# Attention scores in two stacked 128-row passes and four 32-row products per pair of q tiles

## The chip, the core and the metric

The kernel runs on one core of a Trainium2 chip. The metric is the time of one execution on the device in microseconds (us), the median of several runs. The engines are named as in the profile: PE multiplies matrices (PEld is its load of the stationary operand), DVE and ACT work on vectors, POOL does slower vector work, SP issues DMAs. They run side by side, each through its own queue in order, and wait for each other at semaphores.

## What is computed

A two-layer encoder of 1024 tokens and width 1024. Each layer has a mixer (latent attention of 8 heads beside a gated convolution module) and a gated feed-forward part with a short convolution. The change touches the attention:

```python
def block(args):
    qn, qr = args
    sc = (jnp.einsum("bqhd,bkhd->bhqk", qn, k_nope)
          + jnp.einsum("bqhr,bkr->bhqk", qr, k_rope))
    p = jax.nn.softmax(sc.astype(jnp.float32) * scale, axis=-1).astype(v.dtype)
    return jnp.einsum("bhqk,bkhd->bqhd", p, v)
```

`q_nope` and `k_nope` have 64 values a head, the rotary parts `q_rope` and `k_rope` 32, and `k_rope` is shared by the heads; values have 64.

## The kernel before

**Halves.** A 32-bit operand goes to PE as two 16-bit halves, a high one and the rest ("hi", "lo"), and a product is the sum of three: hi·hi, hi·lo, lo·hi. A query or key tile of a head is `(128, 2, 1024)`: 96 of its 128 partitions are used (64 nope, 32 rope), axis 1 is the half, and the last axis are the tokens.

**A q tile.** The attention of a layer (`attention`, L1781) takes the 8 heads × 8 blocks of 128 queries as 64 steps. For a step:

- `scores` (L1818): six products of 96 rows and 512 columns fill a score tile `s` of two PSUM banks (1024 keys); then DVE takes the negated maximum `mx` of each row (L1820).
- `expo` (L1828): ACT writes `p`, the exponential, and its row sum. In the profile it is an ACTIVATE and an ACTIVATION_READ_ACCUMULATOR.
- `turn` (L1858): PE transposes blocks of 128 of `p` for a pair of q tiles into one bank `t`; ACT writes the high half `pt` (L1860), DVE the low half (L1861). There are four such banks of work (c = 0 to 3) for a pair.
- `values` (L1880, L1885): products of `pt` with the values into `o`, for a group of two pairs, in four parts c; each has two products of 128 columns, and the last also eight of 64 columns. Then ACT and DVE write `yt` (L1891, L1892).

PSUM has eight banks: two score tiles of two banks each (`wide`), and four single banks (`bank`) for `t`, `o` and the rest.

**Order.** The loop over `n` writes the order of every engine by hand. A step has, on PE, `values` of an earlier group, `turn(n)`, and the scores of step n + 2; behind these comes `expo(n + 1)`. Lambdas in `agenda[n]` hang other work on a step: the sums of a head (`sums`: PE transposes the sums, L1903, DVE inverts them, L1905, and two DMAs spread them over 64 partitions, L1906, L1907), the multiplication of `y` with them on POOL, and pieces of the tail. Rows of `v` (`rows`, L1794 to L1807) are made ahead of and in the first steps. Taps of the convolution on POOL (L2056 to L2061), with their DMAs, lie beside the whole.

**Loads.** Head 0's tiles come straight from the projections (`DIRECT = 1`); the others pass through DRAM (`qd`, `qrd`, `kd`, `krd`). `load_head` moves a head's query and key tile with 5 DMAs on SP, called while the third q tile of the head before is scored. All such moves go through `move`, L153.

**The end.** The last pair's transposes stand behind nine projection products (`early`, L1026), and the inverse sums of the last head are made by `inverse` (L322, four transposes each).

## Time and profile before

| | |
|---|---|
| median of three runs | 2181.45 us (2181.19 to 2181.64) |
| span of the profiled execution | 2179.0 us |
| first attention: first score product to the last pair's transposes | 200.07 to 391.98 us |
| second attention: the same | 1280.91 to 1472.83 us |

The profile is of one execution. Its list of groups takes a source line, an engine and an operation together; the timeline lists instructions in order of start, with runs of one kind merged (x6: six of them, and the length is from the first start to the last end; lengths of single products are modelled and overlap the next). "[0.30 <-DVE mx L1820]" means that the engine had been idle for .30 us, ended by that instruction. The windows view adds up busy time within a stretch; the DMA view counts a stretch's packets and bytes by queue. `SPq` rows are DMAs as SP issues them; their length is that of the issue.

### The profile page before, as it was taken

The numbers are of one execution on the slowest core, as the hardware profiler recorded it, in microseconds if no ns is written. First come the engines' busy times: TensorE is split into PE (matmuls) and PEld (weight loads), VectorE is DVE, ScalarE is ACT, GpSimd is POOL, SyncE is SP. The second block draws the span as 40 slices with busy tenths as digits, with TensorE's granted clock in tenths as the row PEclk, the third lists the DMA queues.
The fourth block names the chain that finished last, engine by engine and source line by source line (L and its number), as shares of the span: only waits on it lengthen the run. The fifth ranks groups of instructions, "written<-read, shape, count | busy, mean of one in ns | idle before, by whom it ended". The sixth has DMA issues, their size and how long they took to land.

```text
span 2179.0 us, 29766 instructions
## 1 busy us (share of the span) xinstructions
PE 2169.7 (100%) x10722; PEld 1260.7 (58%) x10722; DVE 1844.7 (85%) x2531; ACT 1456.6 (67%) x2183; POOL 537.2 (25%) x534
## 2 busy tenths in 40 slices
PE   9999999999999999999999999999999999999998
PEld 8887665754444444644488876667544444446445
DVE  6989999879998887887859789998898888878877
ACT  6455888746898886554623668886478888865544
POOL 1223777211111111000012355771112111110000
PEclk9999999999999999999999999999999999999999
DMA  6898878754688885554578986886646888856533
GB/s 195 184 187 212 164 152 171 245 163 104 149 244 259 222 261 145 193 178 151 166 177 164 188 207 134 159 186 200 175 100 164 261 241 242 241 141 218 182 111 122
DMA packets 163013, 400.96 MB, mean 184 GB/s; under 512 B 21888, under 2 KB 29936, under 8 KB 162864
## 3 DMA queue, kind: packets, MB, share of 16 engines
q0 software_dynamic: 62528, 145.89, 36.4%
q1 hardware_dynamic: 100048, 252.63, 33.8%
q8 instruction: 84, 1.38, 0.3%
q10 hardware_dynamic: 288, 0.53, 0.1%
q14 instruction: 65, 0.53, 0.1%
HBM read 270.75 MB, written 69.66 MB: 156 GB/s over the span
## 4 chain that ended last, share of the span: by engine, by line
PE 98%; ACT 1%; DVE 1%; issue 0%; DMA 0%; DVEq 0%; ACTq 0%
PE p L1306 36%; PE pd L1551 18%; PE po L1026 7%; PE s L1818 7%; PE t L1858 5%; PE pq L245 3%; PE pa L245 3%; PE o L1880 2%; PE pkv L245 2%; PE pg L245 2%; PE pg L564 2%; PE pn L245 2%; PE o L1885 1%; PE pv L1794 1%; PE pk L245 1%; PE pa L564 1%
## 5 line engine op out<-in xcount | busy, mean ns | idle before, releaser
L1306 PE MATMUL p<-b,w 128*128 128x512 f16 x3696 | 800.0, 379 | 0.2
L1306 PEld LDWEIGHTS <-w 128*128 128x128 f16 x3696 | 358.7, 98 | 431.9 <-issue 0.8
L1551 PE MATMUL pd<-ab,wd 128*128 128x512 f16 (+2 forms) x1920 | 404.2, 373 | 0.0
L1196 POOL DMA_DIRECT2D wu<-in_w_up x176 | 152.2, 879 | 770.2 <-DVE w L1270 581.5
L1551 PEld LDWEIGHTS <-wd 128*128 128x128 f16 x1656 | 161.9, 98 | 179.4 <-issue 0.5
L1818 PE MATMUL s<-k,q 96*128 96x512 f16 x768 | 186.9, 379 | 0.0
L1270 DVE SCALAR_TENSOR_TENSOR w<-wu,wf,w 128x512 f16<-128x512 f32 (+1 forms) x216 | 177.2, 834 | 3.6 <-ACT w L1267 3.6
L1861 DVE SCALAR_TENSOR_TENSOR pt<-t,pt 128x512 f16<-128x512 f32 x256 | 163.0, 676 | 10.0 <-ACT pt L1860 9.0
L1267 ACT ACTIVATE w<-wu,wf 128x512 f16<-128x512 f32 (+1 forms) x216 | 164.8, 781 | 0.1
L1860 ACT ACTIVATE pt<-t 128x512 f16<-128x512 f32 x256 | 139.1, 596 | 32.0 <-PE t L1858 30.0
L1820 DVE TENSOR_REDUCE mx<-s 128x1 f32<-128x1024 f32 x128 | 155.0, 1211 | 1.0 <-PE s L1818 1.0
L1540 ACT ACTIVATE ab<-ac,ds 128x512 f16<-128x512 f32 x108 | 75.5, 717 | 108.7 <-DVE ac L1455 73.0
L1828 ACT ACTIVATE p<-s,mx 128x1024 f32<-128x1024 f32 x128 | 143.3, 1120 | 2.2 <-DVE mx L1820 1.8
L2039 DVE SCALAR_TENSOR_TENSOR conv<-gate,par,conv 128x1009 f32<-128x1009 f32 (+14 forms) x110 | 139.9, 1274 | 3.1 <-ACT conv L659 0.4
L2056 POOL TENSOR_SCALAR late<-gate,par 128x1019 f32<-128x1019 f32 (+13 forms) x99 | 135.5, 1368 | 27.2 <-PE pn L245 13.9
L1858 PE MATMUL t<-ident,p 128*128 128x128 f32 x1024 | 136.6, 275 | 0.9 <-ACT p L1828 0.6
L1858 PEld LDWEIGHTS t<-ident,p 128*128 128x128 f32 x1024 | 116.8, 141 | 34.8 <-issue 7.4
L1766 DVE SCALAR_TENSOR_TENSOR o<-zg,par,o 128x1023 f32<-128x1023 f32 x88 | 112.7, 1281 | 8.9 <-ACT o L1760 7.4
L1314 DVE SCALAR_TENSOR_TENSOR zg<-p,wf,zg 128x512 f32<-128x512 f32 x72 | 54.0, 750 | 71.2 <-PE p L1306 61.6
L1766 DVE SCALAR_TENSOR_TENSOR v<-zv,par,v 128x1023 f32<-128x1023 f32 x88 | 112.1, 1276 | 0.0
L1818 PEld LDWEIGHTS <-q 96*128 96x128 f16 x768 | 74.0, 97 | 64.6 <-issue 2.1
L1541 DVE SCALAR_TENSOR_TENSOR ab<-ac,ds,ab 128x512 f16<-128x512 f32 x108 | 79.9, 748 | 19.2 <-ACT ab L1540 19.2
(2179 smaller groups left out, 3814.1 us busy)
## 6 DMA issues: line engine op xcount, KB each, us to landing
wu<-in_w_up SPq DMA_DIRECT2D x98, 512.0 KB
wu<-in_w_up POOLq DMA_DIRECT2D x176, 256.0 KB, 4.8
sd<-in_w_down SPq DMA_DIRECT2D x44, 512.0 KB
ws<-sd SPq DMA_DIRECT2D x44, 512.0 KB
act<-v SPq DMA_DIRECT2D x36, 512.0 KB
ac<-act SPq DMA_DIRECT2D x72, 256.0 KB
wo<-in_w_o POOLq DMA_DIRECT2D x32, 256.0 KB, 7.7
x_mix<-y SPq DMA_DIRECT2D x32, 256.0 KB
```

Of the source, the lines that this page charges most:

```text
L245: nc.tensor.matmul(ps[:, HALVES[c]], w, x[:, HALVES[c]], start=(k == 0 and s == 0), stop=(k == n - 1 and s == 2))
L1026: self.nc.tensor.matmul(ps, p[:, sl], q[:, cs], start=(k == 0 and t == 0), stop=(k == 3 and t == 2))
L1196: nc.gpsimd.dma_start(out=dst, in_=src, accum_op=ALU.add)
L1267: nc.scalar.activation(out=t, in_=src, func=AF.Copy, scale=scale[f])
L1270: nc.vector.scalar_tensor_tensor(out=t, in0=src, scalar=scale[f], in1=hi, op0=ALU.mult, op1=ALU.subtract)
L1306: nc.tensor.matmul(ps, w[p][:, k * 128:(k + 1) * 128], b[:, q], start=(i in (1, 5, 2) and k == 0 and t == 0), stop=(k == 3 and t == 2), sk ...
L1551: nc.tensor.matmul(ps[t, m][:, cs], w[i, j][p][:, m * 128:(m + 1) * 128], b[:, q, cs], start=(i in (1, 5, 2) and j == 0 and s == 0), stop= ...
L1766: self.nc.vector.scalar_tensor_tensor(out=o[:, a:b], in0=z[:, at + a:at + b], scalar=self.par[l][:, tap:tap + 1], in1=o[:, a:b], op0=ALU.m ...
L1818: nc.tensor.matmul(ps[:, cs], q[0:96, i, qs], k[0:96, j, cs], start=(s == 0), stop=(s == 2))
L1820: nc.vector.tensor_reduce(out=mx, in_=ps, op=ALU.max, axis=AX.X, negate=True)
L1858: nc.tensor.transpose(tp[:, i, qi * 128:(qi + 1) * 128], st["p"][2 * qp + qi][:, kt * 128:(kt + 1) * 128], self.ident)
L1861: nc.vector.scalar_tensor_tensor(out=lo, in0=tp, scalar=P_SCALE, in1=hi, op0=ALU.mult, op1=ALU.subtract)
```

## The change

1. **Scores.** A pair of q tiles takes the even and the odd block of 128 of two neighbours. Keys are stacked: pass 0 has the 64 nope rows of k_hi and below them those of k_lo, both against q_hi; pass 1 has k_hi nope against q_lo and, in the lower 64 rows, rope halves interleaved. Each pass is two products of 512 columns for a q tile: four of 128 rows instead of six of 96. What is left, q_rope hi by k_rope lo, is a product of 32 rows for each tile and half of the keys: four per pair, in four groups of 32 rows (`rest`, L1867). The first tile's two end its sum, the second tile's two begin it.
2. **Order.** The loop runs over pairs. `begin` scores the next pair (first tile whole, then the four small products), the second tile's four products of 128 rows follow later as `second`; `largest` (L1878), `expo` (L1886), `turn` (L1904), `upper` (ACT, L1912) and `lower` (DVE, L1916) are called one by one.
3. **Tiles.** Two key tiles last for a layer (`keys[h % 2]`), with their rope rows loaded once. The tile `rest` (kq) has three slots for query rope rows and one for keys; a DVE copy (`again`, L2066) doubles a head's rows there. Queries lie by parity of their block (`by_parity`).
4. **Loads.** A head is loaded with 11 DMAs (now L159) instead of 5; two heads are direct.
5. **Sums.** They are inverted as 128x8 on DVE (L1954) without a transpose, written to DRAM in that order, and read with strides where `y` is multiplied; they hang on step 8h + 8.

The diff, without lines of like kind:

```diff
-DIRECT = 1
+DIRECT = 2
...
-Y_DELAY = 6
+Y_DELAY = 3
+SUMS_AT = 8
...
+ROWS_FIRST, ROWS_SECOND, ROWS_THIRD = (0, 1, 2), (3, 4), (5, 6)
+ROWS_LATE = {2: (7,)}
...
+            for i, hl in enumerate(two):
+                mine = hl[0:HALF]
+                for e in range(2):
+                    self.move(heads[0][2][e * ROPE + i * HALF:e * ROPE + (i + 1) * HALF], mine[:, 0, HALVES[e]])
+                for p in range(2):
+                    at = NOPE + i * ROPE + p
+                    self.move(heads[0][0][at:at + ROPE - 1:2, 1], mine[:, p])
...
+    def key_tiles(self, l, krd):
+        self.keys = [self.tmp("m", f"k{l}_{e}", F16, (128, 2, T)) for e in range(2)]
+        self.rest = self.tmp("m", f"kq{l}", F16, (128, 4, 512))
+        for k in self.keys:
+            for p in range(2):
+                self.move(k[NOPE + p:127 + p:2, 1], krd[0])
+        for c in range(2):
+            for e in range(2):
+                g = (2 * c + e) * ROPE
+                self.move(self.rest[g:g + ROPE, 3], krd[1][:, HALVES[c]])
...
+    def load_rope(self, tiles, h, qrd):
+        q, _, qc = tiles
+        for i in range(2):
+            for e in range(2):
+                self.move(qc[e * ROPE + i * HALF:e * ROPE + (i + 1) * HALF], qrd[i, h][:, 0, HALVES[e]])
+        for i in range(2):
+            self.move(q[NOPE + i * ROPE:NOPE + (i + 1) * ROPE, 1], qrd[i, h].rearrange("d p t -> (d p) t"))
+
+    def load_head(self, l, h, qd, qrd, kd):
+        q, k, qc = tiles = self.head_tiles(l, h)
+        for p in range(2):
+            self.move(k[0:NOPE, p], kd[h][:, 0])
+        self.move(k[NOPE:128, 0], kd[h][:, 1])
         self.move(q[0:NOPE], qd[h])
-        for i in range(2):
-            self.move(q[NOPE + i * HALF:NOPE + (i + 1) * HALF], qrd[i, h])
-        self.move(k[0:NOPE], kd[h])
-        self.move(k[NOPE:96], krd)
+        self.move(q[NOPE:128, 0], qd[h][:, 0])
+        self.load_rope(tiles, h, qrd)
         return tiles
...
+        def scores(pair):
+            h, p = divmod(pair, 4)
+            st = state[h]
+            q, k, qc = st["qk"]
+            two = [self.wide(f"s{l}_{h}_{2 * p + e}") for e in range(2)]
+            at = [slice(e * 512 + p * 128, e * 512 + p * 128 + 128) for e in range(2)]
+            st["s"].update({2 * p + e: two[e] for e in range(2)})
+
+            def whole(e):
+                for i in range(2):
+                    for cs in HALVES:
+                        nc.tensor.matmul(two[e][:, cs], q[:, i, at[e]], k[:, i, cs], start=(i == 0 and e == 0),
+                                         stop=(i == 1 and e == 1), skip_group_check=True)
+
+            def rest():
+                for e in range(2):
+                    for c in range(2):
+                        r = slice((2 * c + e) * ROPE, (2 * c + e + 1) * ROPE)
+                        nc.tensor.matmul(two[e][:, HALVES[c]], qc[r, at[0]], kc[r], start=(e == 1),
+                                         stop=(e == 0), skip_group_check=True)
+
+            whole(0)
+            rest()
+            return lambda: whole(1)
...
-            qs = slice(qt * 128, (qt + 1) * 128)
-            ps = self.wide(f"s{l}_{h}_{qt}")
-            for s, (i, j) in enumerate(((0, 0), (0, 1), (1, 0))):
-                for cs in HALVES:
-                    nc.tensor.matmul(ps[:, cs], q[0:96, i, qs], k[0:96, j, cs], start=(s == 0), stop=(s == 2))
             mx = self.cp.tile([128, 1], F32, name=f"mx{l}_{h}_{qt}", tag="mx", bufs=4)
-            nc.vector.tensor_reduce(out=mx, in_=ps, op=ALU.max, axis=AX.X, negate=True)
-            st["s"][qt] = ps, mx
+            nc.vector.tensor_reduce(out=mx, in_=st["s"][qt], op=ALU.max, axis=AX.X, negate=True)
+            st["s"][qt] = st["s"][qt], mx
...
+        def upper(pair, c):
+            nc.scalar.activation(out=halves(pair, c)[0], in_=tps[pair, c], func=AF.Copy, scale=P_SCALE)
+
+        def lower(pair, c):
+            hi, lo = halves(pair, c)
+            nc.vector.scalar_tensor_tensor(out=lo, in0=tps.pop((pair, c)), scalar=P_SCALE, in1=hi, op0=ALU.mult, op1=ALU.subtract)
...
+            nc.vector.reciprocal(out=st["sums"], in_=st["sums"])
+            nc.sync.dma_start(out=sd[h].rearrange("(b a) -> b a", a=8), in_=st["sums"])
             nc.sync.dma_start(out=rb[main, :], in_=sd[h:h + 1].partition_broadcast(64))
...
+            agenda[SUMS_AT + 8 * h].append(lambda h=h: sums(h))
...
+        def begin(pair):
+            h, p = divmod(pair, 4)
+            if h >= HEADS:
+                return
+            if p == 0:
+                state[h] = {"sums": self.cp.tile([128, 8], F32, name=f"sums{l}_{h}", tag="sums", bufs=3),
+                            "s": {}, "p": {}, "pt": {}, "qk": loaded.pop(h)}
+            second[pair] = scores(pair)
+            if p == 1 and h + 1 < HEADS and h + 1 not in loaded:
+                loaded[h + 1] = load(h + 1)
+
+        def each(pair, f, *e):
+            if pair < total // 2:
+                f(*e)
+
+        def again(h):
+            qc = loaded[h][2]
+            nc.vector.tensor_copy(out=qc[NOPE:128], in_=qc[0:NOPE])
+
+        for tt in ROWS_FIRST:
+            rows(tt)()
+        again(0)
+        begin(0)
+        ends = [rows(tt) for tt in ROWS_SECOND]
+        largest(0)
+        second.pop(0)()
+        expo(0)
+        for f in ends:
+            f()
+        largest(1)
+        ends = [rows(tt) for tt in ROWS_THIRD]
+        expo(1)
+        for f in ends:
+            f()
+        others(-1)
+        others(0)
+        for pair in range(total // 2 - 1):
+            n, nxt = 2 * pair + 1, pair + 1
+            products(n)
+            begin(nxt)
+            turn(pair, 0)
+            upper(pair, 0)
+            turn(pair, 1)
+            upper(pair, 1)
+            largest(2 * nxt)
+            ends = [rows(tt) for tt in ROWS_LATE.get(n, ())]
+            turn(pair, 3)
+            upper(pair, 3)
+            second.pop(nxt)()
+            lower(pair, 0)
+            largest(2 * nxt + 1)
+            expo(2 * nxt)
+            lower(pair, 1)
+            for f in ends:
+                f()
+            others(n)
+            products(n + 1)
+            ends = [rows(tt) for tt in ROWS_LATE.get(n + 1, ())]
+            turn(pair, 2)
+            upper(pair, 2)
+            expo(2 * nxt + 1)
+            lower(pair, 2)
+            lower(pair, 3)
+            for f in ends:
+                f()
+            others(n + 1)
+            for qi in range(2):
+                state[pair // 4]["p"].pop(2 * (pair % 4) + qi)
+            if pair % 4 == 2 and pair // 4 + 1 < HEADS:
+                again(pair // 4 + 1)
```

On PE in the middle of head 2, before: the end of the scores of q tile 2 (`s_2_2`), an o product pair of head 1, then transposes (`t_2_00` is c = 0 of the head's first pair). "waits" names the engines (or DMA slots) whose counters a row waits for.

```order
L1818 LDWEIGHTS q_2_1978
L1818 MATMUL s_2_2_2253<-k_2_1979,q_2_1978 128x512
L1880 LDWEIGHTS v_2_1625
L1880 MATMUL o_1_1_2236<-pt_00_2138,v_2_1625 128x512
L1880 LDWEIGHTS v_2_1625
L1880 MATMUL o_1_1_2236<-pt_00_2138,v_2_1625 128x512
L1858 MATMUL t_2_00_2276<-ident,p_2_0_2231 128x128 [waits DVE_49]
L1858 MATMUL t_2_00_2276<-ident,p_2_0_2231 128x128
```

A tile's scores are six products in a row, then come o and the transposes. The same place of the changed program: the last product of the first tile of the pair (`s_2_2`), four small ones, the last two of which write the second tile (`s_2_3`), and the transposes.

```order
L1860 MATMUL s_2_2_2289<-k_0_1324,q_2_2012 128x512
L1867 LDWEIGHTS kq_1326
L1867 MATMUL s_2_2_2289<-kq_1326 128x512
L1867 LDWEIGHTS kq_1326
L1867 MATMUL s_2_2_2289<-kq_1326 128x512
L1867 LDWEIGHTS kq_1326 [waits PE_49]
L1867 MATMUL s_2_3_2290<-kq_1326 128x512 [waits Activation_49]
L1867 LDWEIGHTS kq_1326
L1867 MATMUL s_2_3_2290<-kq_1326 128x512
L1904 MATMUL t_2_00_2311<-ident,p_2_0_2262 128x128 [waits DVE_49]
```

The second tile's scores now begin with the small products, which wait for ACT, and the transposes of the pair before stand behind them.

On ACT one pair later, before (`p_2_4` is the exponential of q tile 4 of head 2, `pt` the high halves of the pair ahead of it):

```order
L1860 ACTIVATE pt_00_2281<-t_2_10_2347 128x2x256 [waits PE_49]
L1860 ACTIVATE pt_00_2281<-t_2_11_2354 128x2x256 [waits PE_49]
L1828 ACTIVATE p_2_4_2370,sums_2_2181<-s_2_4_2324,mx_2_4_2331 128x1024 [waits DVE_49,Activation_49]
L1860 ACTIVATE pt_01_2283<-t_2_12_2380 128x2x256 [waits PE_49]
L1860 ACTIVATE pt_01_2283<-t_2_13_2387 128x2x256 [waits PE_49]
L1828 ACTIVATE p_2_5_2403,sums_2_2181<-s_2_5_2361,mx_2_5_2368 128x1024 [waits DVE_49,Activation_49]
```

Before, two high halves stand ahead of each exponential. The same place after:

```order
L1912 ACTIVATE pt_00_2316<-t_2_10_2382 128x2x256 [waits PE_49]
L1912 ACTIVATE pt_00_2316<-t_2_11_2388 128x2x256 [waits PE_49]
L1912 ACTIVATE pt_01_2318<-t_2_13_2396 128x2x256 [waits PE_49]
L1886 ACTIVATE p_2_4_2409,sums_2_2224<-s_2_4_2372,mx_2_4_2394 128x1024 [waits DVE_49,Activation_49]
L1912 ACTIVATE pt_01_2318<-t_2_12_2420 128x2x256 [waits PE_49]
L1886 ACTIVATE p_2_5_2426,sums_2_2224<-s_2_5_2373,mx_2_5_2407 128x1024 [waits DVE_49,Activation_49]
```

Now the first exponential of the pair stands behind three high halves, in the order c = 0, 1, 3, and the second (`p_2_5`) behind that of c = 2.

On SP, the write and read of a head's sums (`sd`, `rb`) and the load of a later head, before:

```order
L1906 DMA sd_1594<-rs_1_2410 8x128 [waits DMAHW7_49,DVE_49]
L1907 DMA rb_0_1818<-sd_1594 64x1024 [waits DMAHW7_49]
L153 DMA q_4_2545<-qd_80 64x2048 [waits DMAHW1_49,PE_49]
L153 DMA q_4_2545<-qrd_81 16x2048 [waits DMAHW2_49]
L153 DMA q_4_2545<-qrd_81 16x2048 [waits DMAHW3_49]
L153 DMA k_4_2546<-kd_82 64x2048 [waits DMAHW4_49]
L153 DMA k_4_2546<-krd_83 32x2048 [waits DMAHW5_49]
```

Five DMAs bring the head's query and key tiles. The same place after:

```order
L1956 DMA rb_0_1846<-sd_1622 64x1024 [waits DMAHW5_49,DMAHW4_49]
L159 DMA k_1_1325<-kd_82 64x1024 [waits DMAHW6_49,PE_49]
L159 DMA k_1_1325<-kd_82 64x1024 [waits DMAHW7_49,PE_49]
L159 DMA k_1_1325<-kd_82 64x1024 [waits DMAHW0_49]
L159 DMA q_3_2299<-qd_80 64x2048 [waits DMAHW1_49]
L159 DMA q_3_2299<-qd_80 64x1024 [waits DMAHW2_49]
L159 DMA kq_1326<-qrd_81 16x512 [waits DMAHW3_49]
L159 DMA kq_1326<-qrd_81 16x512
L159 DMA kq_1326<-qrd_81 16x512 [waits DMAHW5_49]
L159 DMA kq_1326<-qrd_81 16x512 [waits DMAHW6_49]
L159 DMA q_3_2299<-qrd_81 32x1024 [waits DMAHW7_49]
L159 DMA q_3_2299<-qrd_81 32x1024 [waits DMAHW0_49]
```

The load has grown from five rows to eleven behind the sums' read (the write, L1955, stands just ahead); four of them fill `kq`, and the eight slots of the DMA counters now come round within one load. The copy `again` on DVE waits for these four; it stands behind the low halves of the head's third pair and ahead of `yt` and of the next head's first maximum.

More of the change, by code (lines that the diff above doesn't have):

```diff
@@ L911, in project @@
         work(1e9)
-        return u, conv, away, (qd, qrd, kd, krd), (kvs, w["v"], st["scale"], sc), heads
+        return u, conv, away, (qd, qrd, kd), (kvs, w["v"], st["scale"], sc), heads
     def weight_squares(self, l, w, f):
@@ L1967, in attention @@
         state_y = lambda: state[last]["y"]
-        agenda[56].append(lambda: sums(last - 1, slice(0, 64), state[last - 1], state[last - 1]["y"], state[last - 1]["rb"]))
+        for h in range(HEADS - 1):
+            agenda[SUMS_AT + 8 * h].append(lambda h=h: sums(h))
         agenda[60].append(lambda: [self.load_y(l, begun["x"], 0, k) for k in range(2)])
@@ L1985, in attention, with products @@
         agenda[total].append(begun["turn"])
[L1986 to L1988 removed]
+        second = {}
+        def products(n):
             for g, c in chain.get(n, ()):
                 values(g, c, n)
[L1991 to L2011 removed]
@@ L2022, in attention @@
+        pair = total // 2 - 1
+        early(0, range(3))
+        for c in range(4):
+            turn(pair, c)
+            upper(pair, c)
+            lower(pair, c)
+            if c % 2:
+                others(total - 1 + c // 2)
+            if c == 1:
+                early(1, range(2))
+        g = 2 * HEADS - 1
+        values(g, 0, total)
+        values(g, 1, total)
+        early(1, range(2, 3))
+        values(g, 2, total)
+        values(g, 3, total)
         for m in range(2):
```

148 lines of the change are left out of this document (52 added, 96 removed).

## The prediction

> **What bounds the kernel now.** I read the page first: the span, the busy times, and the last chain of work.
>
> ```profile
> span 2179.0 us, 29766 instructions
> PE 2169.7 (100%) x10722; PEld 1260.7 (58%) x10722; DVE 1844.7 (85%) x2531; ACT 1456.6 (67%) x2183; POOL 537.2 (25%) x534
> PE 98%; ACT 1%; DVE 1%; issue 0%; DMA 0%; DVEq 0%; ACTq 0%
> ```
>
> PE never rests, so a microsecond taken from its queue is a microsecond of time, until another engine falls behind it. All that the change touches lies in the two attentions. The windows view (busy us of PE, its weight load, DVE, ACT and POOL, with counts; then the clock, the DMA share and GB/s) gives for most of the first:
>
> ```profile
> 200.00:390.00 190.00, 189.57 (x1164) 115.78 (x1163) 172.07 (x226) 158.18 (x287) 142.49 (x117) 1.00 0.84 175
> ```
>
> PE is full there, but DVE is busy for 172 of 190 us and ACT for 158. Little can be taken from PE before these two decide. Now the steady loop, by the timeline (start, length, engine, line, operation):
>
> ```profile
> 351.97 1.22 DVE L1820 TENSOR_REDUCE mx<-s 128x1 f32<-128x1024 f32 x1
> 352.43 1.08 ACT L1860 ACTIVATE pt<-t 128x512 f16<-128x512 f32 x2
> 352.67 1.46 PE L1818 MATMUL s<-k,q 96*128 96x512 f16 x6
> 353.10 1.28 DVE L1861 SCALAR_TENSOR_TENSOR pt<-t,pt 128x512 f16<-128x512 f32 x2
> 353.40 1.12 ACT L1828 ACTIVATE p<-s,mx 128x1024 f32<-128x1024 f32 x1
> 353.96 0.60 PE L1880 MATMUL o<-pt,v 128*128 128x512 f16 x2
> 354.30 1.22 DVE L1820 TENSOR_REDUCE mx<-s 128x1 f32<-128x1024 f32 x1
> 354.40 0.21 ACT L1828 ACTIVATION_READ_ACCUMULATOR p<-s,mx 128x1 f32 x1
> 354.49 1.05 PE L1885 MATMUL o<-pt,v 128*64 128x512 f16 x8
> 355.48 1.09 PE L1858 MATMUL t<-ident,p 128*128 128x128 f32 x8
> 355.59 0.68 ACT L1891 ACTIVATE yt<-o,sc 64x512 f32<-64x512 f32 x1 [0.98 <-PE o L1885]
> 356.30 0.76 DVE L1892 SCALAR_TENSOR_TENSOR yt<-o,sc,yt 64x512 f32<-64x512 f32 x1 [0.79 <-ACT yt L1891]
> 356.40 1.46 PE L1818 MATMUL s<-k,q 96*128 96x512 f16 x6
> ```
>
> Prices, start to start. Six score products take 353.96 − 352.67 = 1.29, so **.215 each** ("a slot"). Eight transposes after the L1885 products take 356.40 − 355.48 = .92, that is .109 each and about .05 for the changed mode. Two o products and the change to 64 columns take .53, .10 over two slots. Eight 64-column products take .99: they run two abreast, four slots less the last (.65), and then .34 to the next transpose. So entering or leaving a narrow mode costs **about .10 over a slot**. DVE starts the next thing 1.13 after a maximum starts, and .60 after a low half. ACT takes .5 for a high half, and an exponential with its read ends 354.61 − 353.40 = **1.21** after its start. A row of L1885 stands once in a group of four q tiles (two pairs):
>
> ```profile
> 226.27 1.05 PE L1885 MATMUL o<-pt,v 128*64 128x512 f16 x8
> 377.81 1.05 PE L1885 MATMUL o<-pt,v 128*64 128x512 f16 x8
> 387.97 1.05 PE L1885 MATMUL o<-pt,v 128*64 128x512 f16 x8
> ```
>
> From the first to the fourteenth are 13 groups in 151.54, **11.66 each**.
>
> **What the change takes from PE.** A pair had 12 score products; now it has 8 and four of 32 rows. If the four run side by side, as the 64-column pairs do, they take one slot, and one change of mode on each side. That saves 3 × .215 − .2 = .45 per pair, .9 per group, some 14 us per attention.
>
> **Who is late next.** Maxima, high and low halves and exponentials are as many as before; but a pair's two score tiles fill all four score banks, so the new pair's second tile (its two 32-row products start the bank) waits until the old pair's second exponential has read it. In before, a stall of PE on an exponential shows what such a handover costs:
>
> ```profile
> 219.87 1.11 ACT L1828 ACTIVATE p<-s,mx 128x1024 f32<-128x1024 f32 x1 [0.30 <-DVE mx L1820]
> 220.88 0.19 ACT L1828 ACTIVATION_READ_ACCUMULATOR p<-s,mx 128x1 f32 x1
> 221.13 0.87 PE L1858 MATMUL t<-ident,p 128*128 128x128 f32 x6 [0.29 <-ACT p L1828]
> ```
>
> PE starts .06 after the read ends. Now one pair, from the start R of the second tile's 32-row products (0). PE: mode .31, twelve transposes (.05 more for the first) to 1.68, the second tile's four products, the last starting at 2.33 and ending (.38 long) at 2.71. DVE: maximum 2.76 to 3.98. ACT meanwhile: three high halves (1.00, 1.50, 1.99), the first exponential 2.47 to 3.56; the fourth high half at 3.61, since its transposes come only after two o products (2.98 to 3.41) and end .3 later; it is through at 4.09. Both routes then meet: the second exponential can start at 4.0 by DVE and at 4.09 by ACT, ends at 5.30, and the next R is **5.36**. PE's own work to there (16 transposes 1.80, 8 products 1.72, 4 o products .86, the 32-row slot with its two changes of mode .41) is **4.79**: it idles .57. In every second pair the L1885 products stand ahead of R: 4.79 + .10 + .65 + .34 = **5.88**, later than 5.36, so PE decides. A group is 5.36 + 5.88 = **11.24 instead of 11.66**: less than half of what PE saves. DVE then ends its third low half at 2.76 + 1.13 + 1.8 = 5.69, just in time for the next pair.
>
> **The DVE copy**, once per head, doubles the query rows right behind those low halves, and the next head's 32-row products wait for it. Its price is between the nearest rows, a 9-column copy (in the list of groups) and the 64x512 row above (.76):
>
> ```profile
> L938 DVE COPY sc<-sc0p 128x9 f32<-128x9 f32 x1 | 0.2, 157 | 0.0
> ```
>
> I take .25, nearer to the copy: 5.69 + .25 and .08 to reach PE is 6.02, so .15 late against 5.88, six times between those rows: +.9. At .16 it costs .4, at .76 it costs 4.0. Two casts of ys on ACT fall between those rows:
>
> ```profile
> 349.18 1.05 ACT L227 CAST ys_3h<-yt 128x1024 fp32r<-128x1024 f32 x1
> L208 ACT ACTIVATE wo<-wo 128x512 fp32r<-128x512 f32 x4 | 2.6, 642 | 0.0
> ```
>
> They now stand in the exponentials' chain, where a cast pushes the next R by what is over after ACT's slack before the second exponential (.4 at most): about +.65 each, +1.3. The second row, weight casts of the tail, serves below. The transposes of sums on PE and their 8x128 reciprocals go; the new 128x8 reciprocals are off PE's path.
>
> The 13 groups: 13 × 11.24 + .9 + 1.3 = 148.3, **−3.2**.
>
> **The start.**
>
> ```profile
> 200.07 1.47 PE L1818 MATMUL s<-k,q 96*128 96x512 f16 x6
> 200.63 2.44 DVE L1807 SCALAR_TENSOR_TENSOR v<-pv,sc,v 128x256 f16<-128x256 f32 x6
> 1280.91 1.47 PE L1818 MATMUL s<-k,q 96*128 96x512 f16 x6
> ```
>
> The first 32-row products wait for the copy of head 0, queued on DVE behind six v rows that end at about 203.0: PE stands from 201.0 to 203.3. Much of it is caught up, since in before exponentials and maxima were late here anyway. First scores to first L1885: 26.2 before; I take **+.6** (0 to 1.5).
>
> **The end.**
>
> ```profile
> 391.98 1.12 PE L1858 MATMUL t<-ident,p 128*128 128x128 f32 x8
> 1472.83 1.12 PE L1858 MATMUL t<-ident,p 128*128 128x128 f32 x8
> ```
>
> From the fourteenth L1885 to these transposes of the last pair are 14.17 now. Afterwards: one group of 11.24, four transposes of the tail .44, two o products that come ahead of L1885 there .43, and a weight cast in ACT's chain .64 (12.75); then .65 + .34, four transposes .5, nine projection products of .23 (2.05): 16.3, **+2.1**. What follows is the same in both.
>
> **Sum.** An attention: −3.2 + .6 + 2.1 = −.5; the second has the same span (1472.83 − 1280.91 = 191.92, as 391.98 − 200.07 = 191.91). Two give −1.0. The profiled execution spans 2179.0 and the median of the runs is 2181.45, 2.45 around it: 2178.0 + 2.45 = **2180.5**, no change that a measurement of this kernel can tell (about 0.2%, 4.4 us).
>
> **Rivals.**
>
> *The heads' loads become late (slower).* A load was 5 DMAs on SP and is 11, behind the sums' write and read; then come the copy and the next head's scores. Two loads of before, one undisturbed, one beside the convolution's own transfers:
>
> ```profile
> 269.46 0.27 SPq L1906 DMA_DIRECT2D sd<-rs  x1
> 271.22 0.54 SPq L153 DMA_DIRECT2D q<-qd  x1
> 271.80 1.04 SPq L153 DMA_DIRECT2D q<-qrd  x2
> 316.09 0.27 SPq L1906 DMA_DIRECT2D sd<-rs  x1
> 318.83 0.45 SPq L1907 DMA_DIRECT2D rb<-sd  x1
> 319.38 1.56 SPq L153 DMA_DIRECT2D q<-qd  x1
> 320.98 2.31 SPq L153 DMA_DIRECT2D q<-qrd  x2
> 323.83 1.49 SPq L153 DMA_DIRECT2D k<-krd  x1
> q1 hardware_dynamic: 192, 0.52, 49.6%
> ```
>
> The last row, of the DMA view from 325.4 to 329.8, shows SP's queue still moving .52 MB after its last issue at 325.3: the load took about 10.4 us from 319.38. By bytes it grows from 768 to 960 KB, to 13; by count (1.2 per issue × 11 + 4.4) to 17.6; the undisturbed one by count (.52 × 11 + 4.4) to 10. From the sums' write to the first scores that need the load are three pairs less what passes before the write, about 16.0; 1.8 to 3.3 go before the load starts. So a disturbed load is between just in time and 5 late, and an undisturbed one has 4 to spare. About half of twelve heads are disturbed: 0 to +30, most likely +6, **2186**. The same queue carries ten more pieces at the start, which could add 1.
>
> *The four products don't run side by side.* Nothing in before has 32-row products. In twos, PE's pair grows by .215: 15 of these count in each attention, where PE decides: +6, 2186. One after another, the pair with L1885 grows by .65 and the other passes its chain by .08: +.73 × 15 × 2 = +22, **2202**.
>
> [...]
>
> *PE stays the bound (faster).* If the handover were quicker, or leaving and entering the 32-row mode cost nothing (.2 per pair where PE decides, .2 × 15 × 2 = −6, **2174**), more would be left. Were PE alone to decide, a group would be 4.79 + 5.88 = 10.67, another −.57 × 14 × 2 = −16: 2164. Against it stands the chain above, made of durations that are there in before, and DVE: four maxima, eight low halves and a yt are 4 × 1.13 + 8 × .6 + .67 = 10.0 a group.
>
> [...]
>
> **How the numbers follow.** Forecast, given back by chain, copy, start and end (2176 to 2184): .42. Late loads (2183 to 2211): .27. Products in twos or in turn (2186 to 2202): .11. Faster, PE the bound or cheaper modes (2164 to 2176): .20. Faster by over 0.2% (below 2177.1): .20 and a little of the forecast, .25; slower (above 2185.8): two thirds of the loads, most of the second rival and a little, .32; within: .43. The range leaves out the serial case, the worst loads and the best of the faster: **2167 to 2197**.
>
> **What would show it.** In the profile after: L1885 rows 11.2 to 11.4 apart, 12 where a ys cast stands; PE idle about .6 once in a group, put down to the exponential, ahead of the 32-row products; four of these within .22; the copy ending just behind the next head's first four products. Wrong if the 32-row rows are spaced .2 apart, if the copy is seen waiting for a DMA with PE idle for microseconds once per head, or if PE has no idle time in the loop.

## The result and the profile after

| | before | after |
|---|---|---|
| median of the runs of this comparison | 2181.32 us (2181.18 to 2181.64) | 2221.49 us (2219.49 to 2221.87) |
| span of the profiled execution | 2179.0 | 2219.9 |
| first attention: first scores to the last pair's transposes | 200.07 to 391.98 | 202.91 to 415.38 |
| second attention | 1280.91 to 1472.83 | 1305.00 to 1514.38 |

The changed kernel takes 1.0181 times as long, with a 95% interval of 1.0167 to 1.0196. That is slower by 40, where 2180.5 had been forecast and 2197 was the upper end of the range.

The page of after, the same three lines that the prediction began with:

```profile
span 2219.9 us, 29937 instructions
...
PE 2173.6 (98%) x10708; PEld 1247.2 (56%) x10708; DVE 1855.9 (84%) x2547; ACT 1454.7 (66%) x2183; POOL 540.8 (24%) x534
...
PE 86%; ACT 5%; DMA 3%; SPq 3%; DVE 2%; issue 1%; DVEq 0%; ACTq 0%
```

PE was the chain to 98%; now DMA and SP's issues have 6% of it between them. PE's busy time did not fall either (2173.6 against 2169.7), although it does less work. The windows view (busy us of PE, weight load, DVE, ACT, POOL, then granted clock, DMA share, GB/s) tells why, over the same 190 us as in the prediction and in three short stretches:

```profile
200.00:390.00 190.00, 171.09 (x1028) 97.72 (x1028) 159.39 (x211) 138.62 (x253) 133.38 (x109) 0.96 0.80 165
207.20:213.20 6.00, 5.99 (x16) 4.07 (x17) 2.10 (x3) 2.05 (x4) 4.86 (x5) 0.50 0.96 283
262.20:264.40 2.20, 1.93 (x4) 0.25 (x4) 1.04 (x2) 0.00 (x0) 0.00 (x0) 0.50 0.00 0
264.40:268.60 4.20, 4.20 (x21) 3.11 (x21) 1.92 (x2) 1.97 (x4) 0.00 (x0) 0.58 0.00 0
```

PE idles 19 of 190 us, where it had idled .4, and behind its long stalls it works at half its clock. The waits view of PE from 200 to 395 us (what waited, for what, us in total, times, the longest) names what it idles for:

```profile
PE s L1860 <- DMA q<-qrd: 6.5, 4, 2.9
PE s L1867 <- DVE kq L2066: 4.8, 3, 3.0
PE s L1867 <- ACT p L1886: 3.2, 14, 0.6
PE s L1860 <- DMA q<-qd: 3.1, 1, 3.1
```

The third of these is the handover of score banks, which the forecast's sum had. The second is the copy, which the sum had at .9 in a layer's loop and inside the .6 of its start. The first and the fourth are heads' loads that come late; these stood outside the sum, as a rival. One late head, in the timeline of after (start, length, engine, line, operation):

```profile
258.09 1.05 PE L1937 MATMUL o<-pt,v 128*64 128x512 f16 x8
262.21 1.01 PE L1860 MATMUL s<-k,q 128*128 128x512 f16 x2 [3.07 <-DMA q<-qd]
263.03 0.29 DVE L2066 COPY kq<-kq 64x512 f16<-64x512 f16 x1 [3.12 <-DMA kq<-qrd]
263.48 1.01 PE L1860 MATMUL s<-k,q 128*128 128x512 f16 x2 [0.26 <-DMA q<-qrd]
264.42 0.61 PE L1867 MATMUL s<-kq 32*128 32x512 f16 x4
264.97 2.82 PE L1904 MATMUL t<-ident,p 128*128 128x128 f32 x12
271.76 1.53 PE L1904 MATMUL t<-ident,p 128*128 128x128 f32 x12
```

PE had finished with the 64-column products at 262.21 − 3.07 = 259.14 and stood until 262.21. Then the clock is halved (.50 and .58 in the rows from 262.20 and 264.40): twelve transposes take 2.82, where the next pair needs 1.53. The group that holds this stall is 17.29 long (L1937 to L1937) instead of 11.28: 3.3 of standing and 2.7 of slow work. SP's issues for this load (the length is that of the issues):

```profile
243.27 0.32 SPq L1955 DMA_DIRECT2D sd<-sums  x1
249.52 0.47 SPq L1956 DMA_DIRECT2D rb<-sd  x1
250.08 3.10 SPq L159 DMA_DIRECT2D k<-kd  x3
253.24 2.52 SPq L159 DMA_DIRECT2D q<-qd  x2
255.81 4.18 SPq L159 DMA_DIRECT2D kq<-qrd  x4
260.03 0.98 SPq L159 DMA_DIRECT2D q<-qrd  x2
```

From the sums' write to PE's need are 259.14 − 243.27 = 15.87 (16.0 in the prediction). But 6.8 of it go by before the first piece of the load is issued, since the read of the sums waits for their write, and eleven issues and the last landing take 13.4 more. In the five late heads of the two layers 3.5 to 6.8 go by before the first piece, and PE's wait ends 18.9 to 20.2 after the sums' write.

The start of the first attention, from the timeline of after, with DVE and POOL beside PE:

```profile
202.91 1.02 PE L1860 MATMUL s<-k,q 128*128 128x512 f16 x4 [0.66 <-issue]
203.11 2.44 DVE L1846 SCALAR_TENSOR_TENSOR v<-pv,sc,v 128x256 f16<-128x256 f32 x6
204.68 2.33 POOL L2172 TENSOR_TENSOR conv<-conv,late 128x1020 f32<-128x1020 f32 x1
205.58 1.58 DVE L2066 COPY kq<-kq 64x512 f16<-64x512 f16 x1
207.21 0.61 PE L1867 MATMUL s<-kq 32*128 32x512 f16 x3 [2.96 <-DVE kq L2066]
```

The copy that took .29 above takes 1.58 here, and ends at 207.16, .15 behind POOL's instruction (207.01). In the list of groups (by shape; ns are least, median and most) its sixteen executions are:

```profile
L2066 DVE COPY kq<-kq x16: 285/726/1910, 205.6 to 1484.4; 64x512 f16<-64x512 f16 x16
```

Eleven of the sixteen began during an arithmetic instruction of POOL or met one, and each ended .14 to .15 us after that instruction; the five that met none, or only POOL's issue of a DMA, took .28 to .29. So a copy ends .29 after its start or, where POOL computes, .15 after POOL's instruction.

**Where the 40.9 of the span came from**, by the two traces: the first scores come 2.84 later in the first layer. From there to the first L1937 row of a full group it takes 31.1 and 29.8 instead of 26.2, together +8.5. The 13 groups take 164.98 and 163.26 instead of 151.54, +25.2. The end takes 16.38 twice instead of 14.17, +4.4. These make 40.9.

### The profile page after: what moved, and what is told of

Same layout as the page of the kernel before. It is cut to its first block, busy times and chain, and to the rows that moved or that the text cites. A ratio compares the mean times of both kernels' runs of the same rounds, so it can differ in the third digit from the quotient of the medians.

```text
span 2219.9 us, 29937 instructions
## 1 busy us (share of the span) xinstructions
PE 2173.6 (98%) x10708; PEld 1247.2 (56%) x10708; DVE 1855.9 (84%) x2547; ACT 1454.7 (66%) x2183; POOL 540.8 (24%) x534
## 4 chain that ended last, share of the span: by engine, by line
PE 86%; ACT 5%; DMA 3%; SPq 3%; DVE 2%; issue 1%; DVEq 0%; ACTq 0%
PE p L1324 35%; PE pd L1569 18%; PE po L1044 7%; PE t L1904 3%; PE pq L251 3%; PE pa L251 3%; ACT p L1886 2%; SPq L159 2%; PE pkv L251 2%; PE pg L251 2%; PE s L1860 2%; ACT pt L1912 2%; PE pn L251 1%; DMA q<-qrd 1%; PE pg L570 1%
## 5 line engine op out<-in xcount | busy, mean ns | idle before, releaser
L1324 PE MATMUL p<-b,w 128*128 128x512 f16 x3696 | 800.0, 379 | 0.2
L1324 PEld LDWEIGHTS <-w 128*128 128x128 f16 x3696 | 358.8, 98 | 431.8 <-issue 0.8
L1912 ACT ACTIVATE pt<-t 128x512 f16<-128x512 f32 x256 | 140.0, 597 | 86.6 <-PE t L1904 86.1
L1878 DVE TENSOR_REDUCE mx<-s 128x1 f32<-128x1024 f32 x128 | 155.4, 1214 | 29.7 <-PE s L1860 19.6
L1288 DVE SCALAR_TENSOR_TENSOR w<-wu,wf,w 128x512 f16<-128x512 f32 (+1 forms) x216 | 177.2, 834 | 3.6 <-ACT w L1285 3.6
L1916 DVE SCALAR_TENSOR_TENSOR pt<-t,pt 128x512 f16<-128x512 f32 x256 | 165.0, 683 | 9.4 <-ACT pt L1912 7.3
L1860 PE MATMUL s<-k,q 128*128 128x512 f16 x512 | 136.3, 387 | 17.2 <-DMA q<-qrd 11.8
L1886 ACT ACTIVATE p<-s,mx 128x1024 f32<-128x1024 f32 x128 | 143.2, 1119 | 14.7 <-DVE mx L1878 14.4
L1904 PE MATMUL t<-ident,p 128*128 128x128 f32 x1024 | 141.2, 282 | 1.7 <-DVE pt L1916 1.6
L1904 PEld LDWEIGHTS t<-ident,p 128*128 128x128 f32 x1024 | 117.8, 144 | 31.8 <-issue 12.3
L1230 ACT ACTIVATE wsq<-wu 128x1024 f16<-128x1024 f32 x88 | 92.1, 1047 | 0.0
```

The lines of the kernel that those rows point to most:

```text
L1288: nc.vector.scalar_tensor_tensor(out=t, in0=src, scalar=scale[f], in1=hi, op0=ALU.mult, op1=ALU.subtract)
L1324: nc.tensor.matmul(ps, w[p][:, k * 128:(k + 1) * 128], b[:, q], start=(i in (1, 5, 2) and k == 0 and t == 0), stop=(k == 3 and t == 2), sk ...
L1860: nc.tensor.matmul(two[e][:, cs], q[:, i, at[e]], k[:, i, cs], start=(i == 0 and e == 0), stop=(i == 1 and e == 1), skip_group_check=True)
L1878: nc.vector.tensor_reduce(out=mx, in_=st["s"][qt], op=ALU.max, axis=AX.X, negate=True)
L1886: nc.scalar.activation(out=p, in_=ps, func=AF.Exp, bias=mx, accum_out=st["sums"][:, qt:qt + 1])
L1904: nc.tensor.transpose(tp[:, i, qi * 128:(qi + 1) * 128], st["p"][2 * qp + qi][:, kt * 128:(kt + 1) * 128], self.ident)
```

## The experiments

Theory A: heads' loads are late, and each long stall brings a stretch of half clock with it. A1, a part of it: the sums, written as 128 short rows, hold up the loads behind them. Theory C: the DVE copy waits for POOL, again with half clock behind long waits. B stands for rivals under which an earlier load would change little. In the last experiment the question is the start. Differences to before are taken from before's runs in the same comparison (medians 2181.24 to 2182.18).

**1. A load one pair earlier** (issued while the head's first pair is scored, and so ahead of the sums of the head before).

```diff
-            if p == 1 and h + 1 < HEADS and h + 1 not in loaded:
+            if p == 0 and h + 1 < HEADS and h + 1 not in loaded:
```

> The load of the next head is issued one pair earlier, when the head's first pair is begun, ahead of the sums' write and read on SP. Theory A (late loads, and the half clock that follows each long stall of PE, make the loss): PE no longer waits for q<-qd, q<-qrd or the copy's DMAs at head ends, the 13 groups from the first L1937 to the fourteenth take 149 to 151 us in each attention instead of 165 and 163, the granted clock in the loop is 1.00, and what is left is the start and the end: about 2195 us (2190 to 2200). Rival B (the packed scores and their chain are slow themselves): groups stay near 12.6 on average and the time above 2212.

Measured: 2200.77 (2199.54 to 2202.37), 1.0087 times before (1.0072 to 1.0102), 18.6 more than before in place of 40.2, and just above the range that was expected. The 13 groups take 152.87 and 154.84, a little over the expected 151. In the first layer's waits of PE (200 to 395 us) no DMA is left; the two longest are:

```profile
PE s L1867 <- DVE kq L2066: 6.8, 4, 3.9
PE s L1867 <- ACT p L1886: 3.9, 16, 0.6
```

So about half of the loss, 21.6, was A, and what is left names the copy.

**2. The sums transposed on PE again**, inverted as 8x128 and written as eight rows, as in before; the load stays late.

```diff
-            nc.vector.reciprocal(out=st["sums"], in_=st["sums"])
-            nc.sync.dma_start(out=sd[h].rearrange("(b a) -> b a", a=8), in_=st["sums"])
+            pr = self.bank(f"sr{l}_{h}", (8, 128))
+            nc.tensor.transpose(pr, st["sums"], self.ident)
+            rs = self.cp.tile([8, 128], F32, name=f"rs{l}_{h}", tag="rs", bufs=2)
+            nc.vector.reciprocal(out=rs, in_=pr)
+            nc.sync.dma_start(out=sd[h].rearrange("(a b) -> a b", a=8), in_=rs)
...
-            cols = lambda t, a=slice(0, 8): t.rearrange("p (b a) -> p a b", a=8)[:, a]
+            cols = rows
```

> Only the sums go back to the old way: transposed on PE, inverted as 8x128, written as 8 rows of 512 bytes. Theory A1 (the write of 128 rows of 32 bytes, 6.2 us from 243.3 until the read could be issued, delays every load behind it): the read is issued 1.2 to 4 us after the write, loads start up to 3 us earlier at the disturbed heads, and the time falls by 8 to 18 us, to about 2208. Rival A2 (the eleven DMAs are too many by themselves): at most 4 us, 2217 or more.

Measured: 2233.03 (one run), 51 over before in place of 40. The way from the write's issue to the read's shrank only from 6.25 to 5.70 in the head shown above. Over the twelve heads that are loaded its mean fell from 3.6 to 2.8 (1.4 to 6.2 in after, 1.2 to 5.7 here). The loads stayed late all the same (groups of 16 to 18.5). The transpose waits for a bank that DVE's low half gives free, in the waits of PE from 200 to 420:

```profile
PE sr L1955 <- DVE pt L1916: 7.8, 7, 1.1
```

A1 fell as the account of the loss: the short rows cost some .8 a head in the mean, and without them loads are late too. Why the write takes so long in some heads stays open. In the new order PE pays 1.1 for each transpose of the sums, so by this one run the change was right to take it out.

**3. The copy as another DVE operation**, in after as it is.

```diff
-            nc.vector.tensor_copy(out=qc[NOPE:128], in_=qc[0:NOPE])
+            nc.vector.scalar_tensor_tensor(out=qc[NOPE:128], in0=qc[0:NOPE], scalar=1.0, in1=qc[0:NOPE], op0=ALU.mult, op1=ALU.max)
```

> The copy that doubles the query rows becomes a multiplication by 1 and a maximum with itself on DVE, same result. Theory C (the 16-bit copy waits until POOL's instruction ends: copies of 1.58 and 1.29 us end at 207.16 and 237.17, POOL's instructions at 207.01 and 237.02; without POOL it takes .29): every one of the 16 now takes .5 to .8 us whatever POOL does, and the time falls by 1 to 5 us, to about 2218. Rival D (it waits for something else, a DMA's write say): lengths of 1.2 us and more remain and the time is within 1 us of 2221.

Measured: 7918.26 (one run). Products of every phase, also far from the attention, took three times as long (1105 ns for those of L1324, 379 in after), while DVE's and ACT's instructions took as long as in after (834 ns for DVE's L1288 in both). The trace has no record of the granted clock, so the 1.00 that it shows says nothing. Why PE was slow is open. The same edit on top of 1 does not do it, so it is hardly the edit, and with PE this slow the time tells nothing of the copy.

**4. The same edit on top of 1.**

> The earlier load and the slower copy together. Theories A and C: about 3 us under the earlier load alone, 2192 (2187 to 2197). If the copy's waits were only a part of the late loads, no difference from the earlier load alone.

Measured: 2206.98 (2204.84 to 2208.52), 1.0112 (1.0095 to 1.0129): 6 worse than with the copy. The group's row:

```profile
L2066 DVE SCALAR_TENSOR_TENSOR kq<-kq x16: 684/1127/2001, 205.2 to 1472.7; 64x512 f16<-64x512 f16 x16
```

Alone it takes .68, and it too is held while POOL computes: the eleven that met POOL's arithmetic ended .54 to .56 behind it. The expected remedy failed, because this form waits for POOL as well.

**5. The copy on ACT**, on top of 1.

```diff
-            nc.vector.tensor_copy(out=qc[NOPE:128], in_=qc[0:NOPE])
+            nc.scalar.copy(out=qc[NOPE:128], in_=qc[0:NOPE])
```

> The earlier load, and the copy of the query rows done by ACT instead of DVE. Theory C (an instruction of DVE with all its operands in SBUF waits until POOL's instruction ends; the multiplication in place of the copy waited too, .68 to 2.00 us): ACT takes .4 to .7 us for each of the 16 whatever POOL does, PE's stalls of 1.1 to 1.5 us ahead of the 32-row products at head ends become .6 or less, and the time falls from 2200.8 to about 2197 (2194 to 2200). Rival D (the copy waits for the DMAs that fill the same tile): lengths up to 1.5 us stay and nothing is gained.

Measured: 2188.55 (2187.7 to 2189.44), 1.0033 (1.0021 to 1.0045), 11 better than 1 and below the range that was expected. All sixteen copies take the same time, and PE's clock stays whole:

```profile
L2066 ACT COPY kq<-kq x16: 616/617/618, 202.7 to 1453.5; 64x512 f16<-64x512 f16 x16
...
200.00:390.00 190.00, 182.34 (x1132) 103.79 (x1131) 166.71 (x223) 159.66 (x291) 142.26 (x114) 1.00 0.85 183
```

This is C by another way: ACT's copy took .62 all sixteen times, with POOL busy for 142.26 of these 190 us. From the first scores to the first L1937 of a full group it now takes 26.5 and 26.6, near the 26.2 of before. The groups with a copy are still .3 to .5 longer, since ACT's exponentials wait behind it.

**6. No copy: all four groups of query rows by DMA**, on top of 1. Fifteen DMAs a head instead of eleven.

```diff
-        for i in range(2):
-            for e in range(2):
-                self.move(qc[e * ROPE + i * HALF:e * ROPE + (i + 1) * HALF], qrd[i, h][:, 0, HALVES[e]])
+        for g in range(4):
+            for i in range(2):
+                self.move(qc[g * ROPE + i * HALF:g * ROPE + (i + 1) * HALF], qrd[i, h][:, 0, HALVES[g % 2]])
...
-        again(0)
...
-            if pair % 4 == 2 and pair // 4 + 1 < HEADS:
-                again(pair // 4 + 1)
```

> The earlier load, and no copy: the other two groups of query rows come by DMA too, 15 DMAs a head instead of 11, and 4 more pieces for head 0. Theory A (what counts is when the loads begin, not how many there are): no stall of PE at head ends, groups of 11.3 to 11.4 but where a ys cast stands (12.4), 13 groups in 149 to 151 us; at the start PE no longer waits for DVE, but for the pieces. 2193 us (2188 to 2198). Rival (fifteen are too many for SP): PE waits for kq<-qrd or q<-qrd at disturbed heads again, 2200 or more.

Measured: 2187.37 (2183.55 to 2189.86), 1.0024 (1.0015 to 1.0034), just below the range that was expected. The 13 groups take 148.98 in both layers, eleven of them 11.28 or 11.36 and two 12.18: these two hold a ys cast. But SP now has more pieces ahead of the first scores, which come at 204.50 behind a stall of 3.3. (The profile puts this wait down to a row of v on DVE; experiment 7 shows that it was the queue.) Head 0's direct moves, not shown, are doubled alike.

**7. Head 0's pieces first**, on top of 6: the writes of the rope rows to DRAM (`qrd`) are issued behind what head 0 needs.

```diff
-                self.move(qrd[i].rearrange("h d p t -> (h d) p t"), hl)
+                spills.append((qrd[i].rearrange("h d p t -> (h d) p t"), hl))
...
                 self.move(heads[h][0][0:NOPE], mine)
+                while spills:
+                    self.move(*spills.pop(0))
```

> As with the rows by DMA, and at the start head 0's pieces of the rope queries are issued as soon as each half is there, ahead of the two large writes to DRAM, which come behind head 0's own query. Theory E (head 0's pieces are late because they queue on SP behind 1 MB of writes, and PE then runs at half clock): the first scores begin within 1 us of before's place after the last v product, PE has no stall over 2 us and no stretch at a granted clock of .5, first scores to first L1937 25.5 to 27.5 us instead of 31 and 29.7. 2184 us (2180 to 2190). If the pieces' own number is what is late, 2190 or more.

Measured: 2184.33 (2182.23 to 2186.7), 1.0014 (1.0005 to 1.0024), as expected. The runs of 6 and 7 overlap, so the size of the 3.0 between their medians is uncertain. The first scores come at 200.64 without a stall. The way to the first L1938 (this kernel's number for L1937) is 28.7 and 28.6, not the 25.5 to 27.5 that was expected: PE now reaches the second pair's small products early, stands 1.5 and 1.7 for an exponential, and in both layers half clock follows (.74 and .59 in the mean of the next 2.5 us), which E had said would be gone.

**8. The ys casts moved by one step**, on top of 7: they hang on steps whose other work stands behind the pair's second exponential, not between its two.

```diff
-Y_LAST = 4
-Y_SPLIT = 8
+Y_LAST = 3
+Y_SPLIT = 7
```

> As before this one, and the three ys casts of a layer move by one step (Y_SPLIT 8 to 7, Y_LAST 4 to 3), from between a pair's two exponentials to behind the second, ahead of a pair without yt. Theory F (a cast there pushes the second exponential and so the next pair's second tile; 12.7 against 11.6 in these groups): all 13 groups 11.2 to 11.4, 147 to 148 us in sum, and 5 to 6 us less than the run with the new start: about 2178 (2174 to 2184), faster than the kernel before. If ACT's place did not matter, no difference.

Measured: 2178.51 (2176.26 to 2180.49), **0.9987 times before (0.9978 to 0.9997)**: faster than both kernels. From the first to the fourteenth of its rows:

```profile
230.12 1.05 PE L1938 MATMUL o<-pt,v 128*64 128x512 f16 x8
377.31 1.05 PE L1938 MATMUL o<-pt,v 128*64 128x512 f16 x8
```

13 groups in 147.19, 11.32 each (147.33 in the second layer), and the end shrinks from 16.38 to 15.46. PE's waits from 195 to 395 us:

```profile
PE s L1868 <- ACT p L1887: 5.5, 17, 1.5
PE t L1905 <- DVE pt L1917: 0.2, 1, 0.2
```

What is left is the handover that the prediction had described, sixteen times, and the wait of 1.5 at the start, which is also for an exponential.

**9. The last rows of v earlier**, on top of 8, so that PE has work in the wait of the start.

```diff
-ROWS_FIRST, ROWS_SECOND, ROWS_THIRD = (0, 1, 2), (3, 4), (5, 6)
-ROWS_LATE = {2: (7,)}
+ROWS_FIRST, ROWS_SECOND, ROWS_THIRD = (0, 1, 2), (3, 4), (5, 6, 7)
+ROWS_LATE = {}
```

> The kernel with the loads early, all query rope rows by DMA, head 0 first and the ys casts moved, with one more edit: the last rows of v (six products, 1.38 us on PE) are made with the two before them, ahead of the second pair's scores, instead of after the first pair's transposes. If the 1.5 us wait for the exponential near 212 and the half clock behind it (twelve transposes 2.50 instead of 1.53, four scores 1.35 instead of .86) cost time by themselves, PE now works through the wait, the transposes take 1.5, and the first L1938 comes 1 to 2.5 earlier in each layer: 2174.5 (2172 to 2177). If the start is bound by ACT and DVE anyway (the casts of the moved rows stand ahead of the first high halves), the wait only moves to the next exponential and the time stays at 2178.5 (2177 to 2180).

Measured: 2179.22 (2178.01 to 2182.6), 0.9991 (0.9982 to 1.0000), no different from 8. The wait of 1.5 is gone and the clock stays at 1.00 (from 212.00 to 216.30), yet the way to the first L1938 is 27.3 and 27.5 (28.6 and 27.5 in 8): ACT now casts six v rows ahead of the first high halves, and PE waits 1.1 for the exponential behind those. The time came out as the rival said, and PE's wait is still for ACT. But the way is 1.3 shorter in the first layer of the profile, as the first theory said, so that ACT and DVE alone bound the start is not shown.

## Why the prediction was wrong

**The loop was right.** Forecast were groups of 11.24 from a chain of 5.36 and PE's own 5.88; undisturbed groups of after are 11.28 and 11.36, and experiment 8 has thirteen in a row, of pairs of 5.45 and 5.90. The idle time stands where it was put, ahead of the second tile's small products, in experiment 8:

```profile
225.62 0.39 PE L1868 MATMUL s<-kq 32*128 32x512 f16 x2
226.18 0.39 PE L1868 MATMUL s<-kq 32*128 32x512 f16 x2 [0.17 <-ACT p L1887]
```

The two starts are .56 apart (.57 forecast). Where nothing is waited for, four start together, in after:

```profile
217.77 0.39 PE L1867 MATMUL s<-kq 32*128 32x512 f16 x4
218.10 1.72 PE L1904 MATMUL t<-ident,p 128*128 128x128 f32 x12
```

All four and the changes of mode fit in .33 up to the transposes, where by slots of .215 they would take .43 in twos and .86 in turn, so the rival in which they run in twos or in turn is out. Less .10 for a change of mode, the .33 leave .23 for them, 1.1 slots: an estimate, as the .10 is read from other products.

**The end was right**: +2.1 forecast, 16.38 − 14.17 = +2.2 measured. A **ys cast** was priced .65 and cost .9 (12.18 in experiments 6 and 7, 11.28 for the same groups in experiment 8; at the end, 16.38 against 15.46). Moving the casts gained 5.8 in all, where four in the loops at .65 and two at the end at .64 had been forecast to cost 3.9.

**The step that failed first is the price of the rival "the heads' loads become late".** Its mechanism and its place were what came, and so was about the number of late heads: five of twelve stand out in after's groups. The deadline was right as well (15.9 measured in the head shown, 16.0 worked out), and so was the load itself (13.4 to 15.7 from the first issue to the end of PE's wait in the five late heads, 13 to 17.6 forecast). Two sizes were wrong. "1.8 to 3.3 go before the load starts": in the late heads it was 3.5 to 6.8, since the write of the sums took 2.9 to 6.2 before the read could be issued. The trace of before already had 1.8 to 4.6 at its ten loads, of which the prediction had read two. So the lateness, "between just in time and 5 late" and most likely 1 a head (+6 in all), was 2.3 to 3.3 at each of the five. And the stall was counted alone, without the half clock. Against the same groups of experiment 6, the head whose stall of 2.65 left the clock whole lost 2.8, the three with one stretch of 3.4 us at half clock 4.4 to 4.6, and the head shown, with two, 6.0. Experiment 1 puts the whole at 21.6, inside the rival's 0 to +30 but far from its +6. The range was cut at 2197, though this rival alone reached 2211.

**The step that failed second is the copy's price, .25, and "it costs 4.0" as its upper bound.** Alone it takes .29, so the nearest row was well chosen; but nothing in the prediction asked what POOL does at that time. POOL is busy for 142 of 190 us in before, most of it with the convolution, and in after eleven of sixteen copies ended only behind its arithmetic. In experiment 1, groups with a copy that met no arithmetic of POOL are .3 longer than those of experiment 6 without copies, twice the forecast's .15, and groups with a held one up to 1.6; the 13 groups lose 3.9 and 5.9 by the copies, where .9 was forecast. At the start, "PE stands from 201.0 to 203.3" and "+.6" became a stall of 2.96 and half clock behind it. Experiment 6, without copies, gains 12.5 over 1, and experiment 7 another 3.0 by the order of SP's issues at the start (the prediction's "could add 1"; experiment 6 had itself added pieces there).

**The sum of the pieces**: 21.6 (loads), 15.5 (copies and start) and 5.8 (casts) are 42.9; after is 40.2 slower than before, and experiment 8 is 2.7 faster. Of these, the forecast had 3.9 for casts and, with .9 and .6 in each layer, 3.0 for copies and start. The gain that it saw in the loop was there: 151.54 − 147.19 = 4.35 a layer, of which start and end give back most.

## What to carry to other kernels

A load that is late by 3 us can cost twice that where PE is the bound (in after, the stall of 3.07 cost 6.0), so the slack of every load that gets longer or is queued behind another has to be worked out from issue to landing, at the busiest place, and the load issued one step earlier if it is short. A small helper on DVE's critical path is priced with what POOL is doing at that time (the copy took .29 without POOL's arithmetic and up to 1.91 beside it), and tried on ACT or in the DMA where POOL is busy (11 and 12.5 better here, experiments 5 and 6 against 1). When PE's work shrinks by reordering, look at what stands between two links of the chain that then decides: moving three casts a layer by a step was worth 5.8.

## What the runs showed of the hardware

**The granted clock after a stall.** In after and experiments 1, 4, 6, 7 and 8, all eight stalls of PE of 2.9 to 3.9 us were followed by a clock of .50 in the next 2.5 us, and none of fifteen stalls of .9 to 1.4. In between it went both ways (in after, .50 behind a stall of 2.76 and 1.00 behind one of 2.65), and in experiment 2 a stall of 3.01 was followed by .73. So length alone does not decide. The clearest pair is the wait at the start of experiment 8, the same place in its two layers:

```profile
212.23 0.39 PE L1868 MATMUL s<-kq 32*128 32x512 f16 x2 [1.52 <-ACT p L1887]
1292.19 0.39 PE L1868 MATMUL s<-kq 32*128 32x512 f16 x2 [1.72 <-ACT p L1887]
```

The shorter stall was followed by slow work and the longer one was not, and the way to the first L1938 differs by 1.1 (28.58 and 27.47). The records of the clock show where the two differ. In after, the seven stretches of half clock within the attentions are 3.41 us long or, twice, 6.83, and all begin whole multiples of 3.41 us apart: the first three at 206.49, 261.10 and 387.40, 16 and 37 periods apart, and the last at 1486.49, 375 periods behind the first (1280.00 / 375 = 3.413). Two of them, in the windows view again, then the periods around the two waits of experiment 8; there the half clock begins at 213.22, and the edges in the second layer are laid on from it, 315 and 316 periods of 3.413, an estimate:

```profile
206.49:213.32 6.83, 6.11 (x16) 4.08 (x17) 2.77 (x4) 2.09 (x5) 5.69 (x6) 0.50 0.96 270
261.10:267.93 6.83, 5.46 (x21) 3.09 (x22) 2.96 (x4) 1.30 (x3) 0.00 (x0) 0.50 0.09 25
...
209.80:213.22 3.42, 1.90 (x13) 0.95 (x12) 1.42 (x3) 2.24 (x6) 2.30 (x3) 1.00 1.04 213
213.22:216.63 3.41, 3.38 (x13) 2.03 (x12) 3.11 (x6) 2.85 (x6) 3.09 (x4) 0.50 1.05 287
1288.41:1291.83 3.42, 2.06 (x10) 0.78 (x9) 2.49 (x5) 1.29 (x3) 2.87 (x4) 1.00 1.07 212
1291.83:1295.24 3.41, 2.73 (x19) 1.92 (x18) 2.34 (x5) 3.34 (x9) 2.63 (x3) 1.00 1.08 214
```

The stall of 1.52 lies within one period, and the next is at half clock; the stall of 1.72 is cut in two by an edge, 1.36 and .36, and the clock stays whole. In the two attentions of after it comes out alike. Of the periods that began at full clock, none in which PE idled 1.12 us or less was followed by half clock; of the eight others seven were, with 1.48 to 2.70 of idle time, and one with 1.74 was not. That one holds most of the stall of 2.65 (at 337.9), which left the clock at 1.00: an edge cuts it into .91 and 1.74. So in these two runs the half clock goes better with the idle time inside one period than with the length of a stall; what sets it, no run here shows.

**DVE and POOL.** Where they met POOL's arithmetic, the DVE copy of the query rows (in after) ended only .14 to .15 behind it and the two-input operation in its place (experiment 4) .54 to .56, eleven of sixteen times each; the ACT copy (experiment 5) took 616 to 618 ns all sixteen times. The price for the copy is up to 1.6 us on top of .29 (1910 ns, the longest in after). Theory C, as it was put for experiment 5, is too wide: of the reciprocals of the sums on DVE, `sums<-sums`, 128x8, seven began during POOL's arithmetic in after and seven met none, and all fourteen took 191 to 196 ns. Maxima (1172 to 1226 ns) and low halves (672 to 692), which read score banks and `t`, took as long beside POOL as without it. Why the copy waits and these do not, no run here shows.
